# The last 32 tokens of the fetching block, held as four quarters of the channels over 128 partitions

## The chip, the cores and the metric

One core of a Trainium2 chip runs the whole kernel. The metric is the device time of one execution in microseconds (us). TensorE is called PE below (its weight loads PEld), VectorE DVE, ScalarE ACT, GpSimd POOL and SyncE SP, as in the profile.

## What is computed

One decoder block on 256 tokens of 1024 channels, in float32. A state-space mixer and attention are merged and added to x. Then comes the part that matters here, an expert layer (PEER): each token chooses 128 of 16384 experts (8 heads, 16 each), and each expert is one row of a table u and one row of a table v. After it a gated embedding and a final norm close the block:

```python
act = jax.nn.gelu(jnp.einsum('td,thkd->thk', hc, u_tab[ec]))
return jnp.einsum('thk,thkd->td', gc * act, v_tab[ec])
...
    e = p[i] @ ple_w_proj[i]
    x = x + jax.nn.sigmoid(rmsnorm(x, g_ple[i]) @ ple_w_gate[i]) * e
return rmsnorm(x, g_final)
```

## The kernel before

The 256 tokens are two blocks of 128. Block 0 is computed densely: all 16384 rows of u and then of v pass through PE, as 128 tiles of 128 rows each, and unchosen experts have weight zero. Block 1 fetches: for each of its tokens an indirect DMA from POOL's queue (`fetch_rows`, line 687) brings that token's 128 chosen rows, one to a partition.

The change lies in the second half, the sum over rows of v. `v_tile(e2)` fetches a dense tile on SP's queue and multiplies it with two matmuls into the PSUM banks `acc[0]`. `v_chosen(s)` fetches the rows of four tokens, 32q + s for q = 0 to 3, and gives each two matmuls of 512 columns: the weights are 32 columns wide with one column that is not zero, so token 32q + s is added to row s of column strip q of PE, and the four strips run side by side (`tile_position=(0, 32 * q)`). 32 calls cover block 1. A float32 matmul shows as two instructions in the profile. Tiles and rows share one ring of 18 buffers (`RING`), given out in program order.

The loop over the 128 tiles calls `v_chosen` after every third tile from tile 46 on (`ROWS_FROM`, `ROWS_EVERY`), 28 times. Beside tiles up to 61 it also has the selection jobs `g_step` of block 0 (16 small matmuls each, lines 956 and 957), at two tiles the projection `e_part` of the embedding, and from tile 64 on the loads of the gate weights. Four `v_chosen` calls are left behind the loop. They alternate with the five finishing steps of block 0: `turn_x` twice (transposes of x), `norm_x`, `gated` twice (a gate of 512 columns each: 8 matmuls, tanh, multiply-adds, the squares for the final norm) and `finish` (scaling and output DMA). Then `settle(1)` adds the sums of block 1 to x, and the same five steps run for block 1 with nothing beside them.

`rms` makes each reciprocal root: small DVE operations around one `pow` on POOL (line 1099), whose queue also issues the row fetches. PE's order is the program's (`in_turn`); the order on the other engines is set by the scheduler from its own simulated times, and `rms` runs under `tc.high_priority()`.

## Time and profile before

| what | us |
|---|---|
| median of 3 runs (lowest, highest) | 992.03 (991.92, 995.79) |
| the profiled execution, its own time | 990.05 |
| span of that execution, first to last instruction | 988.3 |
| busy in the span: PE, DVE, ACT, POOL | 922.6, 461.2, 160.6, 315.2 |
| loads on SP's queue q1 and on POOL's queue q0, MB | 178.02, 134.26 |

The span is what the trace shows; the execution's own time has 1.75 us around it. A busy PE includes waits inside a run of matmuls, so its share says little by itself; what ends a wait says more. Instructions are read with the line of the kernel, the operation, and what is written <- what is read.

### The profile page before, as it was taken

What the parts mean: (1) busy time and instruction counts of PE and PEld (TensorE: products, weight loads), DVE (VectorE), ACT (ScalarE), POOL (GpSimd) and SP (SyncE); (2) the same over time, 40 slices, a digit from 0 to 9 for tenths busy, and PEclk for the clock granted to TensorE, in tenths of its full rate; (3) what the DMA queues carried; (4) which work ended last, traced back from release to release, by engine and by line L of the source; (5) the groups of instructions that cost most, each with busy time, mean ns of one, the idle gap of its engine ahead of it and who ended that gap; (6) DMA issues with size and microseconds to landing.
All of it is one profiled execution on the core that took longest, in us unless ns stands there. A gap on an engine that the chain in (4) does not pass through costs nothing.

```text
span 988.3 us, 10506 instructions
## 1 busy us (share of the span) xinstructions
PE 922.6 (93%) x3594; PEld 495.0 (50%) x3594; DVE 461.2 (47%) x1338; ACT 160.6 (16%) x336; POOL 315.2 (32%) x353
## 2 busy tenths in 40 slices
PE   6889999999999999679999999889995999999996
PEld 5436777888756754234555545434431333233332
DVE  5787692322654789983466778752100000000023
ACT  6524442011321223201111000000000000000003
POOL 2022121011054532253323466533432443344611
PEclk9999999999999999879999999999998999999999
DMA  9333225922389999999999999999999999999931
GB/s 342 135 104 108 101 79 201 410 78 86 102 294 407 409 408 409 390 338 411 409 409 407 377 398 409 410 409 409 409 409 409 410 409 409 409 409 409 409 152 42
DMA packets 86948, 314.52 MB, mean 318 GB/s; under 512 B 9824, under 2 KB 9840, under 8 KB 86640
## 3 DMA queue, kind: packets, MB, share of 16 engines
q1 hardware_dynamic: 49392, 178.02, 46.8%
q0 software_dynamic: 36928, 134.26, 34.4%
q10 hardware_dynamic: 576, 1.59, 0.5%
q8 instruction: 28, 0.46, 0.2%
q14 instruction: 24, 0.20, 0.1%
HBM read 312.78 MB, written 1.05 MB: 318 GB/s over the span
## 4 chain that ended last, share of the span: by engine, by line
PE 65%; DMA 23%; DVE 8%; ACT 2%; issue 2%; POOL 0%; POOLq 0%; SPq 0%; DVEq 0%; ACTq 0%
PE sp L724 18%; PE va L1011 12%; DMA dn<-in_v 10%; DMA sel<-in_v,rowV 9%; PE va L1021 6%; PE q2p L773 5%; PE zp L126 5%; DMA dn<-in_u 3%; PE nat L452 3%; PE wop L126 3%; PE gp L1136 2%; PE psp L126 1%; PE pap L126 1%; PE gps L957 1%; PE gps L956 1%
## 5 line engine op out<-in xcount | busy, mean ns | idle before, releaser
L687 POOL DMA_INDIRECT sel<-in_urow,rowU x128 | 154.0, 1203 | 250.4 <-PE sp L724 81.5
L724 PE MATMUL sp<-dn,hn 128*128 128x512 f32 x512 | 228.7, 598 | 0.4 <-DMA dn<-in_u 0.2
L687 POOL DMA_INDIRECT sel<-in_v,rowV x128 | 120.3, 940 | 179.9 <-DMA sel<-in_v,rowV 70.4
L734 DVE SCALAR_TENSOR_TENSOR sel<-sel,h1n 128x1024 f32<-128x1024 f32 x128 | 154.6, 1250 | 43.6 <-DMA sel<-in_urow,rowU 29.6
L724 PEld LDWEIGHTS sp<-dn,hn 128*128 128x128 f32 x512 | 95.8, 192 | 109.2 <-issue 102.9
L1011 PE MATMUL va<-dn,SA 128*128 128x512 f32 x256 | 119.6, 605 | 7.8 <-DMA dn<-in_v 7.7
L1021 PE MATMUL va<-sel,C 128*32 128x512 f32 x512 | 99.2, 598 | 5.5 <-DMA sel<-in_v,rowV 5.4
L998 DVE TENSOR_TENSOR x_n<-x_n,va 128x512 f32<-128x512 f32 x4 | 2.7, 685 | 211.7 <-PE va L1011 211.7
L1011 PEld LDWEIGHTS va<-dn,SA 128*128 128x128 f32 x256 | 45.7, 191 | 68.6 <-issue 46.9
L1011 PE MATMUL va<-dn,SB 128*128 128x512 f32 x128 | 61.3, 624 | 10.1 <-DMA dn<-in_v 10.1
L1021 PEld LDWEIGHTS va<-sel,C 128*32 128x32 f32 x512 | 24.5, 109 | 72.5 <-issue 53.0
L126 PE MATMUL zp<-hT,nat 128*128 128x256 f32 x256 | 58.0, 382 | 0.5 <-DVE gat L549 0.5
L773 PE MATMUL q2p<-hn,dn 128*128 128x256 f32 x256 | 57.8, 379 | 0.0
L1011 PE MATMUL va<-dn,SC 128*128 128x512 f32 x128 | 57.8, 600 | 0.0
L726 ACT ACTIVATE sn<-sp,rst 128x512 f32<-128x512 f32 x32 | 22.0, 689 | 185.4 <-PE sp L724 185.3
L126 PEld LDWEIGHTS zp<-hT,nat 128*128 128x128 f32 x256 | 47.7, 190 | 8.3 <-DVE gat L549 0.9
L773 PEld LDWEIGHTS q2p<-hn,dn 128*128 128x128 f32 x256 | 47.5, 190 | 5.8
L452 PE MATMUL nat<-nat,hT 128*128 128x512 f32 x96 | 46.0, 633 | 2.8 <-ACT qk L457 2.8
L1011 PEld LDWEIGHTS va<-dn,SB 128*128 128x128 f32 x128 | 24.1, 197 | 47.0 <-issue 32.5
L943 DVE TENSOR_TENSOR ohl<-oq,gTl 128x512 f16<-128x512 f16 x32 | 13.5, 423 | 73.0 <-PE gps L956 72.8
L416 POOL TENSOR_TENSOR wc<-wc,ws 128x512 f32<-128x512 f32 x8 | 10.3, 1291 | 110.4 <-DVE ws L415 102.3
L1011 PEld LDWEIGHTS va<-dn,SC 128*128 128x128 f32 x128 | 23.5, 190 | 34.2 <-issue 34.2
(285 smaller groups left out, 1024.1 us busy)
## 6 DMA issues: line engine op xcount, KB each, us to landing
dn<-in_u SPq DMA_DIRECT2D x128, 512.0 KB, 11.0
dn<-in_v SPq DMA_DIRECT2D x128, 512.0 KB, 15.6
nat<-in_w_in SPq DMA_DIRECT2D x31, 512.0 KB, 3.3
dn<-in_wq SPq DMA_DIRECT2D x16, 512.0 KB, 10.1
nat<-in_wout SPq DMA_DIRECT2D x8, 512.0 KB, 10.2
g<-in_gate SPq DMA_DIRECT2D x8, 512.0 KB, 20.1
nat<-in_patt SPq DMA_DIRECT2D x4, 512.0 KB, 3.2
nat<-in_pssm SPq DMA_DIRECT2D x4, 512.0 KB, 7.2
```

What stands on the lines that cost most here:

```text
L126: nc.tensor.matmul(ps[:, :T], w[:, k, j * P:(j + 1) * P], a[:, k, :], start=(k == 0), stop=(k == kc - 1))
L416: nc.gpsimd.tensor_tensor(hc[:, :, 0, :], hc[:, :, 0, :], hs_[:, :, 1, :], ALU.subtract)
L452: nc.tensor.matmul(acc[t], hT[:, c, ts], pc[:, k, :], start=(c == 0), stop=(c == DC - 1))
L687: nc.gpsimd.indirect_dma_start(out=sel, out_offset=None, in_=src_d, in_offset=bass.IndirectOffsetOnAxis(ap=rows, axis=0))
L724: pe[0] = nc.tensor.matmul(ps, hn[:, c, :P], w[:, k, :], start=(c == 0), stop=(c == DC - 1))
L726: nc.scalar.activation(sn, ps, AF.Gelu_apprx_tanh, scale=rst2[:, 0:1])
L734: nc.vector.scalar_tensor_tensor(sel, sel, 1.0, h1n, ALU.mult, ALU.mult, accum_out=dots[:, j:j + 1])
L773: pe[0] = nc.tensor.matmul(ps[:, :T], w[:, k], hn[:, k], start=(k == 0), stop=(k == DC - 1))
L943: nc.vector.tensor_tensor(ol, oq, over(gTl, w), ALU.mult)
L1011: pe[0] = nc.tensor.matmul(acc[0][d], s_slot(e2), nat[:, d * 512:(d + 1) * 512], start=(e2 == 0), stop=(e2 == NE - 1))
L1021: pe[0] = nc.tensor.matmul(acc[1][d][32 * q:32 * q + 32, :], C3[:, 32 * t:32 * t + 32], rows[q][:, d * 512:(d + 1) * 512], start=(s == 0), ...
L1136: pe[0] = nc.tensor.matmul(ps, hf[:, c, ts], w[:, c % 2, :], start=(c == 0), stop=(c == DC - 1))
```

## The change

The last 32 tokens of block 1 (`LATE`) leave the groups. `v_chosen` now fetches for three strips, 96 tokens, and is called 23 times over the tiles from 46 on (`CHOSEN_BY`) and nine times behind the loop, beside the finishing steps of block 0. Then `settle(1)` and the five finishing steps of block 1 deal with 96 tokens; they stand among 32 calls of the new `v_late`, one step to every fourth call (`LATE_EVERY`). `v_late` fetches one token's rows and adds them with four matmuls of 256 columns, one to each column strip: quarter q of the channels of late token s lands in row 32q + s of a 256-wide sum. `late()` then finishes these 32 tokens in that shape: add, two transposes, gate (32 matmuls of 256 columns on four strips), final norm, scaling, four output DMAs. A norm now needs a sum over the four quarters, which is a matmul with the constant matrix `same`. What this shape needs of x, of the embedding and of the final gain (`x_q`, `e_q`, `g_q`) is made or loaded beside the dense tiles. One multiplication by the gain that ran on POOL for block 1 (line 1142) goes to DVE.

```diff
-ROWS_EVERY = 3
+LATE = 32
+NP = [P, P - LATE]
+CHOSEN_BY = 23
+Q_BY = 70
+LATE_EVERY = 4
...
         def v_chosen(s):
-            rows = [fetch_rows(v_rows, rowV[:, 32 * q + s:32 * q + s + 1]) for q in range(4)]
+            rows = [fetch_rows(v_rows, rowV[:, 32 * q + s:32 * q + s + 1]) for q in range(3)]
             with in_turn():
                 for d in range(2):
-                    for q in range(4):
+                    for q in range(3):
...
+        acc_l = psV1.tile([P, 512], F32, name="val")[:, :256]
+
+        def v_late(s):
+            t = P - LATE + s
+            rows = fetch_rows(v_rows, rowV[:, t:t + 1])
+            with in_turn():
+                for q in range(4):
+                    pe[0] = nc.tensor.matmul(acc_l[32 * q:32 * q + 32, :], C3[:, 32 * t:32 * t + 32],
+                                             rows[:, q * 256:(q + 1) * 256], start=(s == 0), stop=(s == LATE - 1),
+                                             tile_position=(0, 32 * q))
...
+            ps = psG.tile([P, 512], F32, name="ep", tag="gps")
+            with in_turn():
+                for k in range(2):
+                    for q in (2 * i, 2 * i + 1):
+                        pe[0] = nc.tensor.matmul(ps[32 * q:32 * q + 32, :256], pT[:, k, T - LATE:],
+                                                 w[:, k, q % 2 * 256:q % 2 * 256 + 256], start=(k == 0), stop=(k == 1),
+                                                 tile_position=(0, 32 * q))
+            qs = slice(64 * i, 64 * i + 64)
+            nc.scalar.activation(e_q[qs], ps[qs, :256], AF.Copy)
+
+        def x_quarters():
+            ps = psG.tile([P, 512], F32, name="xqp", tag="gps")
+            with in_turn():
+                for c in range(DC):
+                    q = c // 2
+                    pe[0] = nc.tensor.matmul(ps[32 * q:32 * q + 32, c % 2 * P:c % 2 * P + P], xT[:, c, T - LATE:], ident,
+                                             start=True, stop=True, tile_position=(0, 32 * q))
+            nc.scalar.activation(x_q, ps[:, :256], AF.Copy)
...
-            if e2 >= ROWS_FROM and (e2 - ROWS_FROM) % ROWS_EVERY == 0:
+            while chosen < (e2 + 1 - ROWS_FROM) * CHOSEN_BY // (NE - ROWS_FROM):
                 v_chosen(chosen)
                 chosen += 1
+            if e2 == Q_BY:
+                x_quarters()
...
+                for q in range(4):
+                    nc.sync.dma_start(g_q[32 * q:32 * q + 32], gfin_d[:, q * 256:(q + 1) * 256].to_broadcast([32, 256]))
+                same = eE.tile([P, 4, 32], F32, name="same")
+                nc.vector.tensor_reduce(same[:, 0, :], ident.rearrange("p (q i) -> p i q", i=32), AX.X, ALU.add)
+                nc.vector.tensor_copy(same[:, 1:, :], same[:, 0:1, :].to_broadcast([P, 3, 32]))
...
+                    ps = psE.tile([P, 512], F32, name="sqp", tag="X")
+                    with in_turn():
+                        pe[0] = nc.tensor.matmul(ps[:, 0:1], same.rearrange("p q i -> p (q i)"), sq_q[:, k:k + 1],
+                                                 start=True, stop=True)
+                    nc.vector.tensor_scalar(v, ps[:, 0:1], 1.0 / D, EPS, ALU.mult, ALU.add)
...
-            (nc.gpsimd if h == 0 and t else nc.vector).tensor_tensor(x_n[:, t, hs], x_n[:, t, hs], g_row[:, hs], ALU.mult)
+            nc.vector.tensor_tensor(x, x, g_row[:np_, hs], ALU.mult)
...
+        def late():
+            nc.vector.tensor_tensor(x_q, x_q, acc_l, ALU.add)
+            jq = eE.tile([P, 256], F32, name="jq")
+            ps = psE.tile([P, 512], F32, name="xqT", tag="X")
+            with in_turn():
+                for j in range(2):
+                    pe[0] = nc.tensor.transpose(ps[:, j * P:(j + 1) * P], x_q[:, j * P:(j + 1) * P], ident)
+            nc.scalar.activation(jq, x_q, AF.Square, accum_out=sq_q[:, 0:1])
+            hq = eE.tile([P, DC, LATE], F32, name="hq")
+            nc.vector.tensor_tensor(hq.rearrange("p (q j) i -> p q j i", j=2),
...
+            rms(2 * NT, r1, True)
+            pg = psE.tile([P, 512], F32, name="gpq", tag="A", bufs=2)[:, :256]
+            with in_turn():
+                for c in range(DC):
+                    for q in range(4):
+                        pe[0] = nc.tensor.matmul(pg[32 * q:32 * q + 32, :], hq[:, c, :],
+                                                 gate_w(c, q // 2)[:, q % 2 * 256:q % 2 * 256 + 256],
+                                                 start=(c == 0), stop=(c == DC - 1), tile_position=(0, 32 * q))
+            sg = eE.tile([P, 256], F32, name="sgq")
+            nc.scalar.activation(sg, pg, AF.Tanh, scale=r1)
+            nc.vector.scalar_tensor_tensor(sg, sg, 1.0, e_q, ALU.add, ALU.mult)
+            nc.vector.scalar_tensor_tensor(x_q, sg, 0.5, x_q, ALU.mult, ALU.add)
+            nc.scalar.activation(jq, x_q, AF.Square, accum_out=sq_q[:, 1:2])
+            nc.vector.tensor_tensor(x_q, x_q, g_q, ALU.mult)
+            rms(2 * NT + 1, r2, False)
+            nc.vector.tensor_scalar(x_q, x_q, r2, None, ALU.mult)
+            for q in range(4):
+                (nc.scalar if q % 2 else nc.sync).dma_start(out_d[P - LATE:, 1, q * 256:(q + 1) * 256],
+                                                            x_q[32 * q:32 * q + 32, :])
...
-        steps = [lambda: turn_x(0, 0), lambda: (turn_x(0, 1), norm_x(0)), lambda: gated(0, 0),
-                 lambda: gated(0, 1), lambda: finish(0)]
-        left = 32 - chosen
-        for i in range(max(left, len(steps))):
-            if i < left:
-                v_chosen(chosen)
-                chosen += 1
-            if i < len(steps):
-                steps[i]()
+        todo = steps(0)
+        while chosen < 32:
+            v_chosen(chosen)
+            chosen += 1
+            if todo:
+                todo.pop(0)()
         settle(1)
-        for h in range(2):
-            turn_x(1, h)
-        norm_x(1)
-        for h in range(2):
-            gated(1, h)
-        finish(1)
+        todo += steps(1)
+        for i in range(LATE):
+            v_late(i)
+            if todo and i % LATE_EVERY == LATE_EVERY - 1:
+                todo.pop(0)()
+        late()
```

`settle`, `squares`, `rms`, `turn_x`, `gated` and `finish` take only the first 96 partitions where they deal with block 1.

## Rows read from the trace of the kernel before

**Rows 1.** The page's part 2: the span in 40 equal slices of 24.7 us; the granted clock in tenths of full speed, and the GB/s that the DMA engines moved.

```profile
...
PEclk9999999999999999879999999999998999999999
...
GB/s 342 135 104 108 101 79 201 410 78 86 102 294 407 409 408 409 390 338 411 409 409 407 377 398 409 410 409 409 409 409 409 410 409 409 409 409 409 409 152 42
...
```

**Rows 2.** Busy time by windows around the end. Columns: the window in us, its length, busy us and instruction counts of PE, PEld, DVE, ACT and POOL, granted clock, DMA share, GB/s.

```profile
...
940.00:945.00 5.00, 5.00 (x23) 1.75 (x20) 1.46 (x7) 0.62 (x2) 2.46 (x3) 1.00 1.03 410
...
947.00:948.00 1.00, 1.00 (x3) 0.30 (x2) 0.00 (x0) 0.00 (x0) 0.00 (x0) 1.00 0.71 287
...
950.00:951.00 1.00, 1.00 (x4) 0.47 (x3) 0.00 (x0) 0.00 (x0) 0.00 (x0) 1.00 0.02 8
...
```

**Rows 3.** The row fetches of line 687 between 926 and 942 us: their durations in ns, the first and last start, and the time from issue to landing.

```profile
...
L687 POOL DMA_INDIRECT sel<-in_v,rowV x13: 936/936/938, 926.1 to 941.4; - x13
...
DMA to landing us min/median/max: 9.4/9.5/9.5
```

**Rows 4.** Timeline of POOL in the dense stage and at its end: start, length, line, operation, count, and in brackets the idle time before it and what ended that.

```profile
...
650.00 0.94 POOL L687 DMA_INDIRECT sel<-in_v,rowV  x1 [0.30 <-issue]
...
941.41 0.94 POOL L687 DMA_INDIRECT sel<-in_v,rowV  x1 [0.34 <-issue]
942.38 0.59 POOL L1099 TENSOR_TENSOR r_all<-v,mhalf 128x1 f32<-128x1 f32 x1
...
```

**Rows 5.** Timeline of PE from the last groups of rows to the transposes of block 1, columns as in rows 4.

```profile
...
938.00 4.60 PE L1021 MATMUL va<-sel,C 128*32 128x512 f32 x16
...
947.65 7.13 PE L1136 MATMUL gp<-g,hf 128*128 128x512 f32 x16
954.71 1.94 PE L1021 MATMUL va<-sel,C 128*32 128x512 f32 x16
956.59 7.13 PE L1136 MATMUL gp<-g,hf 128*128 128x512 f32 x16
963.56 1.04 PE L1115 MATMUL x2T<-ident,x_n 128*128 128x128 f32 x8
...
```

**Rows 6.** The chain of work that ended last, pieces in order of time around the first groups of rows: start, length, line, instructions.

```profile
...
677.43 1.87 PE va L1021 x16
679.30 5.35 PE va L1011 x12
...
```

**Rows 7.** Timeline of PE in the state-space stage: the outputs on two column strips (line 430), and what starts behind them.

```profile
...
67.10 1.06 PE L430 MATMUL yp<-wc,cblk 128*32 128x256 f32 x8
68.10 1.09 PE L477 MATMUL qkTp<-ident,qk 128*128 128x128 f32 x8
...
```

**Rows 8.** Groups of instructions by line, form and engine in the first 300 us: operands, count, busy us and mean ns of one, idle time before.

```profile
...
L549 DVE TENSOR_TENSOR gat<-zp,rbc 128x256 f32<-128x256 f32 x16 | 6.6, 416 | 22.8 <-PE zp L126 22.8
...
L259 ACT ACTIVATE xs<-xn 128x256 f32<-128x256 f32 x8 | 3.3, 414 | 0.2
...
L430 PEld LDWEIGHTS yp<-wc,cblk 128*32 128x32 f32 x64 | 3.2, 109 | 5.0 <-issue 3.5
...
L563 ACT ACTIVATE sgl<-glp 128x256 f32<-128x256 f32 x4 | 1.5, 383 | 15.2 <-PE glp L126 15.2
...
L259 ACT ACTIVATION_READ_ACCUMULATOR xs<-xn 128x1 f32 x8 | 1.5, 186 | 0.0
...
L637 DVE TENSOR_SCALAR hn<-xT,gains 128x256 f32<-128x256 f32 x4 | 1.4, 353 | 0.1
...
L139 PE MATMUL ss_ffn<-ones,sq 128*128 128x1 f32 x4 | 0.6, 255 | 1.0 <-ACT sq L144 1.0
...
L139 PEld LDWEIGHTS ss_ffn<-ones,sq 128*128 128x128 f32 x4 | 0.5, 190 | 1.1 <-ACT sq L144 1.1
...
```

**Rows 9.** Timeline of all engines behind the last gate of block 1, columns as in rows 4.

```profile
...
978.79 0.69 ACT L1138 ACTIVATE sg<-gp,r_all 128x512 f32<-128x512 f32 x1 [3.97 <-PE gp L1136]
979.51 0.69 DVE L1139 SCALAR_TENSOR_TENSOR sg<-sg,e_n 128x512 f32<-128x512 f32 x1 [5.45 <-ACT sg L1138]
...
981.03 0.63 ACT L1090 ACTIVATE junk<-x_n 128x512 f32<-128x512 f32 x1 [1.54 <-DVE x_n L1140]
...
983.85 0.72 ACT L1151 ACTIVATE x_n<-x_n,r_all 128x512 f32<-128x512 f32 x1 [2.10 <-DVE r_all L1102]
...
984.60 0.35 ACTq L1154 DMA_DIRECT2D out<-x_n  x1
```

**Rows 10.** Timeline of PE: a selection job (its first instruction, and the tile behind its sixteenth), and the tiles behind the longest wait of the dense stage.

```profile
...
688.28 0.22 PE L956 MATMUL gps<-ohl,o 128*128 128x64 f16 x1
...
689.25 3.67 PE L1011 MATMUL va<-dn,SA 128*128 128x512 f32 x8
...
763.39 7.84 PE L1011 MATMUL va<-dn,SB 128*128 128x512 f32 x12 [9.94 <-DMA dn<-in_v]
...
```

**Rows 11.** Busy time by windows, columns as in rows 2, around that wait and in the stage in which PE waits for single rows.

```profile
...
755.00:760.00 5.00, 0.00 (x0) 0.00 (x0) 0.00 (x0) 0.00 (x0) 0.77 (x1) 0.81 1.02 409
760.00:763.00 3.00, 0.00 (x0) 0.00 (x0) 0.00 (x0) 0.00 (x0) 0.00 (x0) 0.50 1.03 411
...
938.00:943.00 5.00, 5.00 (x21) 1.84 (x20) 0.00 (x1) 0.37 (x1) 3.90 (x5) 1.00 1.03 410
...
```

**Rows 12.** Timeline of DVE: the input of the `pow` of block 0's norm, and what waited for its result.

```profile
...
934.36 0.15 DVE L1098 TENSOR_SCALAR v<-v 128x1 f32<-128x1 f32 x1
943.00 0.16 DVE L1100 TENSOR_TENSOR rs<-r_all 128x1 f32<-128x1 f32 x1 [8.49 <-POOL r_all L1099]
...
```

More of the change, by code (lines that the diff above doesn't have):

```diff
@@ L1070, in block_kernel @@
                 nc.sync.dma_start(pT, pT_d)
+                e_q = eE.tile([P, 256], F32, name="e_q")
+                x_q = eE.tile([P, 256], F32, name="x_q")
+                g_q = eE.tile([P, 256], F32, name="g_q")
+                for q in range(4):
[3 more added lines that the diff above has]
+                nc.vector.tensor_copy(same[:, 1:, :], same[:, 0:1, :].to_broadcast([P, 3, 32]))
                 g_row = eE.tile([P, D], F32, name="g_row")
@@ L1086, in block_kernel @@
         sq_s = eE.tile([P, 2 * NT, 2], F32, name="sq_s")
+        sq_q = eE.tile([P, 2], F32, name="sq_q")
         def squares(t, h, i):
             junk = eE.tile([P, 512], F32, name="junk")
-            nc.scalar.activation(junk, x_n[:, t, h * 512:(h + 1) * 512], AF.Square, accum_out=sq_s[:, i, h:h + 1])
+            np_ = NP[t]
+            nc.scalar.activation(junk[:np_], x_n[:np_, t, h * 512:(h + 1) * 512], AF.Square,
+                                 accum_out=sq_s[:np_, i, h:h + 1])
         def rms(i, r, half):
+            np_ = NP[i % NT] if i < 2 * NT else P
             with tc.high_priority():
-                v = eE.tile([P, 1], F32, name=f"v{i}")
-                rs = eE.tile([P, 1], F32, name=f"rs{i}")
-                nc.vector.tensor_tensor(v, sq_s[:, i, 0:1], sq_s[:, i, 1:2], ALU.add)
-                nc.vector.tensor_scalar(v, v, 1.0 / D, EPS, ALU.mult, ALU.add)
-                nc.gpsimd.tensor_tensor(r, v, mhalf[:, 0:1], ALU.pow)
+                v = eE.tile([P, 1], F32, name=f"v{i}")[:np_]
+                rs = eE.tile([P, 1], F32, name=f"rs{i}")[:np_]
+                r = r[:np_]
+                if i < 2 * NT:
+                    nc.vector.tensor_tensor(v, sq_s[:np_, i, 0:1], sq_s[:np_, i, 1:2], ALU.add)
+                    nc.vector.tensor_scalar(v, v, 1.0 / D, EPS, ALU.mult, ALU.add)
+                else:
+                    ps = psE.tile([P, 512], F32, name="sqp", tag="X")
+                    k = i - 2 * NT
+                    with in_turn():
+                        pe[0] = nc.tensor.matmul(ps[:, 0:1], same.rearrange("p q i -> p (q i)"), sq_q[:, k:k + 1],
+                                                 start=True, stop=True)
+                    nc.vector.tensor_scalar(v, ps[:, 0:1], 1.0 / D, EPS, ALU.mult, ALU.add)
+                nc.gpsimd.tensor_tensor(r, v, mhalf[:np_, 0:1], ALU.pow)
                 nc.vector.tensor_tensor(rs, r, r, ALU.mult)
@@ L1127, in norm_x, with gate_w @@
             rms(t, r_all[:, t:t + 1], True)
+        def gate_w(c, h):
+            return gate[4 * h + c // 2].rearrange("p (k n) -> p k n", k=2)[:, c % 2, :]
         def gated(t, h):
-            ts = slice(t * P, (t + 1) * P)
+            np_ = NP[t]
+            ts = slice(t * P, t * P + np_)
             hs = slice(h * 512, (h + 1) * 512)
-            ps = psE.tile([P, 512], F32, name="gp", tag="A", bufs=2)
+            ps = psE.tile([P, 512], F32, name="gp", tag="A", bufs=2)[:np_]
             with in_turn():
                 for c in range(DC):
-                    w = gate[4 * h + c // 2].rearrange("p (k n) -> p k n", k=2)
-                    pe[0] = nc.tensor.matmul(ps, hf[:, c, ts], w[:, c % 2, :], start=(c == 0), stop=(c == DC - 1))
-            sg = eE.tile([P, 512], F32, name="sg", bufs=2)
-            nc.scalar.activation(sg, ps, AF.Tanh, scale=r_all[:, t:t + 1])
-            nc.vector.scalar_tensor_tensor(sg, sg, 1.0, e_n[:, t, hs], ALU.add, ALU.mult)
-            nc.vector.scalar_tensor_tensor(x_n[:, t, hs], sg, 0.5, x_n[:, t, hs], ALU.mult, ALU.add)
+                    pe[0] = nc.tensor.matmul(ps, hf[:, c, ts], gate_w(c, h), start=(c == 0), stop=(c == DC - 1))
+            sg = eE.tile([P, 512], F32, name="sg", bufs=2)[:np_]
+            x = x_n[:np_, t, hs]
+            nc.scalar.activation(sg, ps, AF.Tanh, scale=r_all[:np_, t:t + 1])
+            nc.vector.scalar_tensor_tensor(sg, sg, 1.0, e_n[:np_, t, hs], ALU.add, ALU.mult)
+            nc.vector.scalar_tensor_tensor(x, sg, 0.5, x, ALU.mult, ALU.add)
             squares(t, h, NT + t)
-            (nc.gpsimd if h == 0 and t else nc.vector).tensor_tensor(x_n[:, t, hs], x_n[:, t, hs], g_row[:, hs], ALU.mult)
+            nc.vector.tensor_tensor(x, x, g_row[:np_, hs], ALU.mult)
         def finish(t):
+            np_ = NP[t]
             r2 = r_all[:, NT + t:NT + t + 1]
@@ new lines, in late @@
+        def late():
[8 more added lines that the diff above has]
+            nc.vector.tensor_tensor(hq.rearrange("p (q j) i -> p q j i", j=2),
+                                    ps[:, :256].rearrange("p (j q i) -> p q j i", j=2, q=4),
+                                    gp.rearrange("p (q j) -> p q j", j=2).unsqueeze(3).to_broadcast([P, 4, 2, LATE]),
+                                    ALU.mult)
+            r1, r2 = (r_all[:, 2 * NT + i:2 * NT + i + 1] for i in range(2))
+            rms(2 * NT, r1, True)
[17 more added lines that the diff above has]
+                                                            x_q[32 * q:32 * q + 32, :])
@@ L1175, in layout @@
+        assert not todo
+        late()
 def layout(inputs):
```

24 lines of the change are left out of this document (15 added, 9 removed).

## The prediction

> **What bounds the kernel now.** I read the slices of the page first, then the windows around the end, then the timelines of each engine there. From the middle of the span on, the traffic stands at 407 to 411 GB/s in most slices, dips in four and falls for good only in the last two, while TensorE's clock stays at its upper level but for short dips [rows 1]. So the second half is paced by DMA: each tile or row fetch moves 128 x 1024 x 4 B = 0.524 MB, 1.28 us at 409 GB/s. The end is different. The traffic is still 410 GB/s at 940 to 945 us, is down to 287 at 947, and the last bytes come at 950 to 951 [rows 2]; the last row fetch is issued at 941.41 and lands 9.4 to 9.5 us later, at 950.9 [rows 3, 4]. From there to the end of the span are 988.3 - 950.9 = 37.4 us with no load left to hide them. The reader is to see in the PE timeline what fills them: gates of block 0, the last group of rows at 954.71, gates of block 0 again, then the whole finish of block 1: transposes at 963.56, 14 us of gate matmuls, then an elementwise chain [rows 5, 9].
>
> **What is removed from behind the last row.** Both gate halves of block 0 and both of block 1 (7.06 us of PE each, as from 947.65 to 954.71 [rows 5]) now stand among the fetches; only 32 tokens, spread as four quarters of the channels over 128 partitions, are finished behind the last row. The sum needs two things: when the last row has gone through PE, and how long the new tail is.
>
> **When the last row is through: the DMA side.** Bytes of rows and tiles are the same, 128 row fetches each time, moved from the dense stage (112 before, 69 after) to behind it (16 before, 59 after). New ahead of the last row are the outputs of block 0 (0.524 MB, 1.28 us) and of 96 tokens of block 1 (0.96 us), which were written behind it before, and four loads of the quartered gain (0.13 MB, 0.3 us): 2.6 us. So the last row lands at 950.9 + 2.6 = 953.5 if the queues stay full, and its own matmuls (0.5, below) with a wait of 0.3 end at 954.3. Will a stage of rows alone stay full? In the stretch 926 to 942 every fetch was a row, 1.28 us apart (0.94 of work and 0.34 idle), landing steadily 9.4 to 9.5 us after issue at 410 GB/s [rows 2, 3, 4]. POOL's shortest step is 0.94 + 0.30 = 1.24 us [rows 4], so it has only 0.04 us a fetch to spare. Four new-placed `pow` operations (norm and finish of either block) of 0.59 us plus 0.3 each take 3.6 us from it; the 9.4 us in flight absorb that, and I cost it at nothing. Without that cover it is 3.6 us. What a waiting `pow` would cost is a rival below. All tiles stand ahead of them on SP's queue, and ACT's issues take 0.35 us each [rows 9], so the moved output DMAs block no load.
>
> **The PE side.** The group of four rows, 16 instructions on four column strips, takes 1.87 us; with three strips each strip still has its four instructions, so a group of three rows costs 1.87 as well, 32 times: 0.62 a row instead of 0.47. A tile takes 5.35 / 3 = 1.783 [rows 6]. A late row is 8 instructions of 256 columns over four strips, two a strip. No row shows this; the nearest is the state-space output, 8 instructions of the same shape on two strips, four a strip, in 68.10 - 67.10 = 1.0 us, 0.25 an instruction [rows 7]. So a late row is 2 x 0.25 = 0.5 us; halving the 512-column group gives 0.47 as the low bound; weight loads strictly one after another, 8 x 0.109 [rows 8], give 0.87 as the high one. I take 0.5, since the same strips overlap in both rows. From the first group at 677.43 PE then has: 81 tiles 144.4; 32 groups 59.8; four selection jobs of 0.97 [rows 10], 3.9; the embedding projection, 16 instructions at 5.35 / 12, 7.1; its quartered copy and the quartered x, three sets like rows 7, 3.0; 16 transposes at 0.13 [rows 5], 2.1; four gates 28.2; 32 late rows 16.0. That is 264.5 us. To it comes one idle stretch of 9.9 with a slow restart of 7.84 - 5.35 = 2.5, which the burst of eight gate-weight loads caused and will cause again [rows 10]: 276.9, so 954.3. The late rows and the quartered copies, 19 us, are new in it; with them the two sides meet. Each will hold up the other now and then (14 us of gates at once leave about 15 of the 18 ring slots landed and unused), so I set the last row's end at 955.5.
>
> **The new tail.** The add from PSUM 0.42, as the 128x256 of VectorE; Square and its read 0.41 + 0.19; the sum over quarters as a 1-column matmul, 0.45 (0.26 and a weight load of 0.19); with 0.2 of handoffs 1.65 until gates may start, the two transposes and their 0.42 copy running beside it [rows 8, 9]. The gate is 64 instructions on four strips, 16 a strip: 16 x 0.25 = 4.0 (bounds 3.7 by rows 6, 7.0 by loads one after another) and 0.1 to start. So 5.75 to its end. From the end of the last gate before, at 978.79, to the end of the span it was 9.5 us [rows 9]. With 256 columns in place of 512, tanh loses 0.31, the two multiply-adds 0.54, Square 0.22, the scaling 0.37 [rows 8, 9]; the gain no longer stands between the sum and its `pow` (0.5 less); the 1-column matmul in place of an add costs 0.4, a second output issue per queue 0.35. That is 8.3. The tail is 14.1 us, the span 955.5 + 14.1 = 969.6, 18.7 less than before.
>
> Added work hidden elsewhere: the `same` matrix, e_q, x_q and their copies, some 2 us of ACT and DVE in stretches where both are near idle, 2 us on the path if that cover went; four SP issues of 0.35, 1.4 us, under up to 18 tiles in flight. The multiplication moved from POOL to VectorE, some 0.69 as its like in rows 9, lies among the rows.
>
> **The clock, and a rule against the change.** The granted clock fell to 0.50, 1.2 of 2.4 GHz, after PE had nothing at all from 753 to 763, and 12 matmuls then took 7.84 us; while PE waited for each row at 938 to 943 it stayed at 1.00 [rows 10, 11]. The Trainium skill, TensorE: Matmul & The Clock Gate, section HAM oscillation, warns that bursts that wait for their DMA each time let the clock fall back; late rows are such bursts. By the trace at 938 to 943 nothing changes and the span is 969.6; by the rule the tail runs at half clock and it is 974.9.
>
> **Rivals.**
> 1. *The clock falls among the late rows*, since 0.5 us of work stands in each 1.28 us, for longer than before. The rows in reach speak against it: 1.87 us of work in 4.6 at 938 to 943 left it at 1.00 [rows 5, 11]. Price: gate + 4.0, last row, transposes and 1-column matmuls + 1.3: 5.3, time 978.6.
> 2. *PE becomes the bound* with late rows at 0.87: 32 x 0.37 = 11.8 on PE, and the gate 7.0: + 3.0. As PE was level with DMA, all of it is seen: 13.6 with the 1.2 us of slack that I gave, time 987. For it: no margin; against: the strips overlap in two shapes.
> 3. *POOL waits inside its queue (the other side).* POOL is in order; if the `pow` of block 0's finish stands ahead of the fetches that follow it in the program, these wait for gates on PE. The first four groups behind the last tile, with the turns and gates between them, take PE some 23 us, the chain to `pow` 3.7, while only about 5 unlanded rows are under way: some 21 us without DMA; block 1's finish adds 7. 28 us against 18.7 gained: 9.3 slower, time 1001. It decides from 18.7 us of idle DMA on. Against it: the `pow` of block 0's norm, ahead of eight fetches in the program, ran at 942.38 behind all of them, though its input was there from 934.5 [rows 4, 12]. A part of it, one `pow` some fetches too early, 5 to 12 us, is likelier: about 981.
>
> **How the numbers follow.** The profiled execution took 990.05, 1.75 above its span; the median of the runs shown, 992.03, is 1.98 above that. So 969.6 gives 971.35 and, as median, 973.3. Chances: forecast 0.62, clock 0.08, PE bound 0.09 (half of it in between, about 980), POOL in part 0.14, POOL in full 0.07. The forecast's own range is 966 (outputs absorbed, a tail 3 us shorter) to 978; the range 966 to 985 holds all but the full cases of rivals 2 and 3. Faster by over 0.5% (5 us, about what a measurement of this kernel can tell) 0.88, within 0.05, slower 0.07.
>
> **What would show it.** Right: traffic near 409 GB/s until about 951 us; 59 row fetches in a row at 1.28 us; late rows of 0.5 us on PE; under 15 us from the last row to the end; clock 1.00 throughout. Wrong: gaps in POOL's fetches ended by VectorE's `v`; traffic that dips among the gates; late rows over 0.8 us; 0.50 in the last 20 us.

## The result, and the profile after

The changed kernel took 987.19 us (median of 10 runs, 982.17 to 989.52), the kernel before 992.74 (10 runs, 989.26 to 995.91): a ratio of 0.995 (0.9928 to 0.9971). Forecast were 973.3 and a range of 966 to 985. The profiled execution took 989.52, the longest of the ten; its span is 987.8, and the forecast span was 969.6.

The page's part 2 of the changed kernel, columns as in [rows 1]:

```profile
...
PEclk9989999999999999879999999999997999999889
...
GB/s 344 147 99 110 90 86 213 409 61 86 109 294 408 409 407 409 392 316 409 409 408 409 382 396 409 409 408 409 409 398 409 403 374 394 410 409 375 310 360 55
...
```

The traffic dips where it was to stand at 409, and the clock is under its upper level near the end. Busy time by windows there, columns as in [rows 2]:

```profile
...
913.00:920.00 7.00, 7.00 (x31) 2.45 (x32) 1.39 (x2) 1.35 (x3) 1.76 (x2) 1.00 0.67 268
920.00:926.00 6.00, 6.00 (x52) 2.38 (x49) 0.83 (x3) 0.06 (x1) 4.47 (x6) 1.00 0.77 236
930.00:946.00 16.00, 10.08 (x32) 2.11 (x32) 0.62 (x3) 1.03 (x4) 10.85 (x12) 0.58 1.02 399
...
```

Among the gates of block 0 the traffic is 268 and 236 GB/s. From 930 to 946 it is full again, yet PE runs 32 instructions in 16 us, and its clock stands at 0.58. The timeline of PE shows these instructions; the columns are those of [rows 4]:

```profile
...
929.00 0.62 PE L1178 MATMUL x2T<-ident,x_n 96*128 96x96 f32 x4 [1.46 <-issue]
930.73 0.59 PE L1039 MATMUL val<-sel,C 128*32 128x256 f32 x2 [1.10 <-issue]
932.19 2.73 PE L1039 MATMUL val<-sel,C 128*32 128x256 f32 x7 [0.87 <-issue]
935.75 1.30 PE L1039 MATMUL val<-sel,C 128*32 128x256 f32 x3 [0.83 <-issue]
937.88 1.05 PE L1039 MATMUL val<-sel,C 128*32 128x256 f32 x2 [0.83 <-issue]
...
946.05 0.55 PE L1178 MATMUL x2T<-ident,x_n 96*128 96x96 f32 x4
...
967.52 7.11 PE L1039 MATMUL val<-sel,C 128*32 128x256 f32 x128
...
976.13 3.66 PE L1245 MATMUL gpq<-g,hq 128*32 128x256 f32 x64
...
```

Four late rows, 32 instructions, lie between the transposes at 929.00 and those at 946.05. Where nothing disturbs them, 128 instructions take 7.11 us (967.52), so 32 should take 1.8. Here they come in pieces of one to nine. The starts are 1.46, 2.13 or 3.56 us apart, all near multiples of 0.71 us, and the idle time before each piece ended by nothing that the profile shows ("issue"). In the runs below I call this *pieces*. ScalarE, too, follows PE late. Its copies of the transposes of 892.31 and of 929.00 (recorded ends 892.97 and 929.62):

```profile
...
900.58 0.37 ACT L1186 ACTIVATE hf<-x2T,gains 128x128 f32<-128x128 f32 x1 [8.57 <-PE va L1027]
...
945.08 0.34 ACT L1186 ACTIVATE hf<-x2T,gains 128x96 f32<-128x96 f32 x1 [14.58 <-PE val L1039]
...
```

They start 7.6 and 15.5 us after them. The Trainium skill, Perfetto Trace Analysis, section Summary: the profiler window per engine type, says that TensorE's record has an estimated end and leaves out the propagation of its semaphore. This trace shows the 7.6 and 15.5 us; whether PE's signal came late or ScalarE's own instruction it does not show.

PE loses time before any late row, too. A group of three rows is 12 instructions and takes 1.8 us where nothing holds it (half of 3.66 at 888.72); the one at 896.40 takes 4.62. Its weight loads wait three times (0.76, 0.29 and 0.44 us), by the profile for rows, yet POOL had issued its three fetches by 881.9, and a fetch landed 9.5 us after its issue in the kernel before [rows 3]. PE's timeline up to the first gate of block 0:

```profile
...
888.72 3.66 PE L1027 MATMUL va<-sel,C 128*32 128x512 f32 x24
892.31 0.66 PE L1178 MATMUL x2T<-ident,x_n 128*128 128x128 f32 x4
...
896.40 4.62 PE L1027 MATMUL va<-sel,C 128*32 128x512 f32 x12
901.00 7.13 PE L1203 MATMUL gp<-g,hf 128*128 128x512 f32 x16
...
```

POOL's timeline in the same stretch:

```profile
...
919.17 0.94 POOL L692 DMA_INDIRECT sel<-in_v,rowV  x1 [5.24 <-PE va L1027]
...
926.67 0.59 POOL L1161 TENSOR_TENSOR r_all<-v,mhalf 128x1 f32<-128x1 f32 x1
...
939.78 0.58 POOL L1161 TENSOR_TENSOR r_all<-v,mhalf 96x1 f32<-96x1 f32 x1
940.53 0.99 POOL L692 DMA_INDIRECT sel<-in_v,rowV  x1 [0.18 <-issue]
...
```

It stops for 5.24 us before 919.17, until PE gives a slot of the full ring free, then fetches every 1.25 us until 940.53. The two `pow` (926.67, 939.78) fit in between without a wait.

Rows end at 967.52 + 7.11 = 974.6 in place of 955.5. The tail behind them is 987.8 - 974.6 = 13.2 in place of 14.1. So the whole miss, 19.1 us, lies ahead of the last row's end.

### The profile page after: what moved, and what is told of

Its sections match the earlier page's. It is cut to its first block, busy times and chain, and to the rows that moved or that the text cites. A ratio compares the mean times of both kernels' runs of the same rounds, so it can differ in the third digit from the quotient of the medians.

```text
span 987.8 us, 11007 instructions
## 1 busy us (share of the span) xinstructions
PE 918.2 (93%) x3824; PEld 498.7 (50%) x3824; DVE 467.3 (47%) x1356; ACT 163.8 (17%) x344; POOL 319.7 (32%) x354
## 4 chain that ended last, share of the span: by engine, by line
PE 75%; DMA 12%; DVE 8%; issue 3%; ACT 2%; POOL 0%; SPq 0%; POOLq 0%; DVEq 0%; ACTq 0%
PE sp L729 19%; PE va L1017 17%; DMA dn<-in_v 9%; PE q2p L778 5%; PE zp L131 5%; PE va L1027 5%; PE gp L1203 3%; PE wop L131 3%; PE nat L457 3%; PE val L1039 2%; PE psp L131 1%; PE pap L131 1%; PE gps L962 1%; PE gps L961 1%; DMA dn<-in_u 1%
## 5 line engine op out<-in xcount | busy, mean ns | idle before, releaser
L692 POOL DMA_INDIRECT sel<-in_urow,rowU x128 | 156.6, 1224 | 248.6 <-PE sp L729 78.4
L692 POOL DMA_INDIRECT sel<-in_v,rowV x128 | 122.6, 958 | 195.6 <-PE va L1017 82.0
L1004 DVE TENSOR_TENSOR x_n<-x_n,va 128x512 f32<-128x512 f32 (+1 forms) x4 | 2.6, 682 | 171.2 <-PE va L1017 170.5
L1027 PE MATMUL va<-sel,C 128*32 128x512 f32 x384 | 63.9, 598 | 0.0
L1027 PEld LDWEIGHTS va<-sel,C 128*32 128x32 f32 x384 | 15.4, 109 | 43.8 <-issue 40.8
```

The costliest lines, as they stand in the source:

```text
L692: nc.gpsimd.indirect_dma_start(out=sel, out_offset=None, in_=src_d, in_offset=bass.IndirectOffsetOnAxis(ap=rows, axis=0))
L1027: pe[0] = nc.tensor.matmul(acc[1][d][32 * q:32 * q + 32, :], C3[:, 32 * t:32 * t + 32], rows[q][:, d * 512:(d + 1) * 512], start=(s == 0), ...
```

## The experiments

The 18 runs came in five groups, each on a chip of its own; I number the chips in that order. The chip of the runs of the result isn't recorded. All ratios are to the kernel before on the same chip. The first theory (pieces come where transposes and gates stand among single rows) had as rivals traffic, the number of instructions, and the full ring.

**First chip: is it the steps among the rows, the instructions, the bytes or the ring?**

*Block 1's steps behind the last late row.*

```diff
-        todo += steps(1)
         for i in range(LATE):
             v_late(i)
-            if todo and i % LATE_EVERY == LATE_EVERY - 1:
-                todo.pop(0)()
...
+        for step in todo + steps(1):
+            step()
```

> The five steps of block 1 (transposes, norm, two gate halves, finish) stand behind the last of the 32 late rows instead of behind every fourth of them. Theory A (TensorE falls behind when it is fed the sixteen narrow instructions of a late row while the traffic is full): the rows that came in pieces in the changed kernel, four in 15 us, come in pieces still, over 1.5 us a row wherever the traffic is above 390 GB/s, and the span is over 1000 us. Theory B (it is the transposes and gates between the rows that make TensorE wait): with none of them between, every late row goes through at the pace at which rows land, 1.25 to 1.3 us, the last one ends near 964, and the span is 964 + 1.5 + 14.3 + 13.5 = about 993. Theory C (only the gates of block 0, 16 us in one go, matter, because the ring fills and the fetches stop): the fetches still stop for 5 us near 913, and rows run as in theory B.

Measured: 992.63 (10 runs), ratio 1.0017 (1.0003 to 1.003). PE, among rows alone:

```profile
...
929.16 0.59 PE L1039 MATMUL val<-sel,C 128*32 128x256 f32 x2 [0.83 <-issue]
...
942.65 6.35 PE L1039 MATMUL val<-sel,C 128*32 128x256 f32 x49 [0.82 <-issue]
...
```

Pieces stand from 926 to 943, and again from 949 to 958, with no transpose or gate among the rows. That theory falls. The rows end at 964.9; the steps behind them cost the rest.

*Half the instructions of late rows 1 to 30 (two strips of four).*

```diff
-                for q in range(4):
+                for q in range(2 if 0 < s < LATE - 1 else 4):
```

> Of each late row but the first and the last, only the strips of two of the four quarters are multiplied (half of the channels of these 30 rows are left out): half of the instructions, the same fetches, transposes and gates. Theory A: the four rows that took 15 us take 4 us or less, the fetches do not wait for TensorE near 943, and the time is 972 to 980 us. Theories B and C: the pieces and their gaps stay, 12 us or more for these four rows, and the time is within 3 us of the changed kernel's 987.

Measured: 980.58 (4 runs), ratio 0.9898 (0.9878 to 0.9918). The time lies between the two that were expected. Pieces stay, from 925.7 to 941. They last as long as before. With half the instructions a row, about five rows pass in them (21 instructions) in place of four, which may be part of why less time is lost.

*Half of the bytes of each late row* (the first half of its channels, by an index doubled beforehand; the two upper strips multiply it once more).

```diff
-            rows = fetch_rows(v_rows, rowV[:, t:t + 1])
...
+            nc.gpsimd.indirect_dma_start(out=rows[:, :512], out_offset=None, in_=v_half,
+                    in_offset=bass.IndirectOffsetOnAxis(ap=rowV2[:, s:s + 1], axis=0))
...
```

> Each late row is fetched with half of its channels (2 KB a partition instead of 4; the second half of the channels is then multiplied with the first half's values). As many fetches and TensorE instructions, but the traffic of this stage falls to about 210 GB/s, since the issue of a fetch takes 1.24 us whatever it moves. Theory A: no pieces, each late row 0.47 us, and the time is 968 to 978 us. Theory B: the pieces stay, since transposes and gates stand where they stood: 980 us or more. Theory C: the fetches still stop near 913 for 5 us, rows run as in theory A.

Measured: 982.91 (4 runs), ratio 0.9925 (0.9901 to 0.995). Busy time by a window in the pieces, columns as in [rows 2]:

```profile
...
930.00:941.00 11.00, 5.50 (x13) 1.86 (x14) 0.14 (x1) 0.00 (x0) 7.30 (x8) 0.50 0.70 203
...
```

13 PE instructions in 11 us at 203 GB/s: full traffic is not the cause.

*Each gate in halves of eight instructions, a group or four rows between them.*

```diff
-            return [..., lambda: gated(t, 0), lambda: gated(t, 1), ...]
+            return [..., lambda: gate_part(t, 0, 0), lambda: gated(t, 0),
+                    lambda: gate_part(t, 1, 0), lambda: gated(t, 1), ...]
```

> Each gate half of 7.1 us is given out in two parts of four accumulation steps, 3.5 us, with a group of rows (or four late rows) between them; nothing else differs. Theory C: the ring never fills, the 5 us without a fetch near 913 are gone, the last row is through 6 to 12 us sooner, and the time is 975 to 981 us. Theory A: TensorE falls behind as before at the late rows, the time is 983 to 989 us. Theory B: two more places where other work stands between rows, 987 us or more.

Measured: 987.73 (10 runs), ratio 0.9986 (0.9966 to 1.0007). POOL's longest stop is 2.86 us in place of 5.24; the pieces stand from 924.7 to 939. The ring is not their cause either, and with it all three theories of this group have fallen.

**Second chip: place in the instruction stream, block 0's finish, who fetches.** One run each.

*64 small matmuls more, long before, so that PE's later instructions move on in its stream.*

```diff
+            if e2 == W0 + 1:
...
+                    for _ in range(64):
+                        pe[0] = nc.tensor.matmul(ps[:, :64], iot4[:, :, 0], iot4[:, :64, 0], start=True, stop=True)
```

> Sixty-four small matmuls (128 instructions with their weight loads) are added near 720 us, where TensorE later waits about 10 us for the gate weights; nothing else changes. In the four experiments before, the stretch in which TensorE's instructions come 0.7 us and more apart began at the same place of its instruction stream, whatever stood there. Theory D (TensorE's instructions themselves come too late, at a place of the stream): the stretch begins 128 instructions earlier in the work, among the groups of three rows near 922 us or it is gone, and late rows 4 to 7 take about 2 us. Theory F (row fetches through POOL's queue, or another thing that hangs on the work itself): it stays at late rows 4 to 7, 12 to 15 us, time as the changed kernel's, 987.

*`finish(0)` behind the last late row.*

```diff
-        todo = steps(0)
+        todo = steps(0)[:4]
...
+        finish(0)
         late()
```

> The finish of block 0 (norm, scaling and its two output DMAs of 256 KB) stands behind the last late row. Theory E (the outputs of block 0, which start at 928 us, where the stretch begins, hold TensorE up): the gaps at late rows 4 to 7 are gone, the rows end near 962, and the time is about 977 with the finish added to the tail's side work. Theories D and F: the gaps stay, 12 to 15 us for these rows, time 986 to 990.

*Late rows as plain tiles on SyncE's queue* (32 consecutive tiles, not the chosen rows).

```diff
-            rows = fetch_rows(v_rows, rowV[:, t:t + 1])
+            rows = fetch_dense(v_d[s])
```

> The 32 late rows are fetched by SyncE as plain tiles of the same size, and from fixed places, not the chosen ones (their values are therefore other ones); POOL then issues nothing among them. Theory F (fetches through POOL's queue hold TensorE up): no gaps, 0.5 us a late row, the time falls to about 972. Theory D: the gaps stay where they are in the stream, 12 to 15 us for rows 4 to 7.

*One strip of four in late rows 1 to 30.*

```diff
-                for q in range(4):
+                for q in range(1 if 0 < s < LATE - 1 else 4):
```

> Of late rows 1 to 30 one quarter of the channels alone is multiplied: 4 instructions a row with the weight loads, in place of 16; same fetches. Theory A, which the run with two strips spoke against: no gaps at all. Theory D: the gaps last as long in instructions as before, some 50 of them 0.3 us each, and so reach over more rows; with 4 instructions a row TensorE still follows the fetches at 1.25 us a row, and the rows end near 964, the time is about 977. Theory F: gaps in the same fetches, near 926 to 942 us, whatever the number of instructions.

Measured: 973.42, 976.47, 972.67 and 977.42, the kernel before 986.89. None of the four has pieces, so nothing here tells what removes them; the chip itself became the suspect. Two things can be read, each from single runs. A quarter of the PE work in late rows 1 to 30 gave no shorter time (977.42 against 973.42 with all of it, the stream shifted), so nothing shows PE as the bound of an undisturbed run. And moving `finish` behind the rows did not help (976.47).

**Third chip: the unaltered kernel again.**

> The changed kernel itself, unaltered, once more. The last four experiments ran on another chip than the four before them, and none of them shows TensorE's instructions coming in pieces, not even the one whose edit stands far from that place. Theory G (the pieces belong to the chip on which the kernel runs, not to the kernel alone): on a chip without them the unaltered kernel takes 973 to 977 us, its late rows 4 to 7 about 2 us; on a chip with them 985 to 989. Theory D alone (the place in the instruction stream, which the added matmuls moved): 985 to 989 with the pieces at late rows 4 to 7, whatever the chip.

> The kernel with 64 small matmuls added near 720 us, once more, beside the unaltered one on the same chip. Theory G: within 2 us of the unaltered kernel beside it, on either kind of chip; where there are pieces they start near the same instruction number or the same row. Theory D: 10 us or more faster than the unaltered one.

> The gate halves given out in two parts, on the same chip as the unaltered kernel. If no pieces disturb TensorE, this edit is tested alone: the fetches then wait less for the ring while the gates of block 0 run (they waited 5.3 us in all in the kernel with the added matmuls), the last row is through 3 to 5 us sooner, near 955, and the time is 2 to 5 us under the unaltered kernel's. With pieces: within 2 us of it.

Measured: the unaltered kernel 975.16 (4 runs, 971.35 to 978.74), ratio 0.9853 (0.9814 to 0.9891); with the stream shifted 976.31 (4), 0.9856; with gates in halves 975.9 (4), 0.986. No pieces in any of them. This is the cleanest result of the study: the same kernel has a span of 972.6 here and 987.8 in the profile of the result. PE of the unaltered kernel on the third chip:

```profile
...
886.76 3.66 PE L1027 MATMUL va<-sel,C 128*32 128x512 f32 x24
890.35 0.66 PE L1178 MATMUL x2T<-ident,x_n 128*128 128x128 f32 x4
...
893.38 1.93 PE L1027 MATMUL va<-sel,C 128*32 128x512 f32 x12
895.24 7.13 PE L1203 MATMUL gp<-g,hf 128*128 128x512 f32 x16
...
928.63 0.64 PE L1039 MATMUL val<-sel,C 128*32 128x256 f32 x8 [1.67 <-DMA sel<-in_v,rowV]
931.32 1.08 PE L1039 MATMUL val<-sel,C 128*32 128x256 f32 x8 [2.05 <-DMA sel<-in_v,rowV]
...
933.61 9.19 PE L1203 MATMUL gp<-g,hf 128*96 128x512 f32 x16
...
958.88 0.64 PE L1039 MATMUL val<-sel,C 128*32 128x256 f32 x8 [0.57 <-DMA sel<-in_v,rowV]
...
961.01 3.66 PE L1245 MATMUL gpq<-g,hq 128*32 128x256 f32 x64
...
```

Each late row is whole, and what ends its wait is its own data. The pieces are gone, and ScalarE no longer follows late; its copies behind the transposes that end at 891.01 and 926.11:

```profile
...
891.04 0.37 ACT L1186 ACTIVATE hf<-x2T,gains 128x128 f32<-128x128 f32 x1 [2.68 <-PE x2T L1178]
...
926.15 0.34 ACT L1186 ACTIVATE hf<-x2T,gains 128x96 f32<-128x96 f32 x1 [0.47 <-PE x2T L1178]
...
```

What is left of the miss shows in the windows and at POOL:

```profile
...
913.00:920.00 7.00, 7.00 (x57) 2.56 (x56) 1.31 (x4) 0.72 (x2) 5.07 (x6) 1.00 0.69 216
920.00:926.00 6.00, 4.57 (x73) 2.73 (x65) 2.96 (x10) 2.73 (x7) 4.89 (x6) 1.00 1.01 333
...
930.00:934.00 4.00, 2.49 (x17) 0.80 (x18) 0.00 (x0) 0.00 (x0) 3.06 (x5) 0.63 1.03 419
934.00:938.00 4.00, 4.00 (x6) 1.23 (x6) 1.16 (x6) 0.34 (x1) 3.21 (x4) 0.52 1.03 410
...
```

```profile
...
913.41 0.93 POOL L692 DMA_INDIRECT sel<-in_v,rowV  x1 [3.80 <-PE va L1027]
...
```

The ring is full behind block 0's gates, POOL stops 3.80 us, and the traffic is 216 and 333 GB/s. Against 409 that is (193 x 7 + 76 x 6) / 409 = 4.4 us of DMA. Behind this gap PE waits 1.67 and 2.05 us for single rows, the clock falls to 0.63 and 0.52, and the gate at 933.61 takes 9.19 in place of 7.11.

With gates in halves (the third kernel of this group) POOL stops for no more than 0.87 us there, and traffic ends at 952, as the forecast had it. It gained nothing:

```profile
...
931.83 5.43 PE L1206 MATMUL gp<-g,hf 128*96 128x512 f32 x6 [3.35 <-DVE hf L1184]
...
953.67 3.66 PE L1039 MATMUL val<-sel,C 128*32 128x256 f32 x64
959.69 0.44 PE L1241 MATMUL xqT<-ident,x_q 128*128 128x128 f32 x2 [2.36 <-DVE x_q L1236]
...
```

The rows end at 957.3, but a gate half waited 3.35 us for its input and ran at half clock, and the tail's first add stood 2.36 us behind the elementwise work of block 1's finish on VectorE.

**Fourth chip: is it the work or its place, and who fetches?**

*Gates in halves, block 1's norm behind the first half, a step to every third late row* (shown against the kernel with gates in halves).

```diff
-LATE_EVERY = 4
+LATE_EVERY = 3
-            return [lambda: turn_x(t, 0), lambda: (turn_x(t, 1), norm_x(t)), lambda: gate_part(t, 0, 0),
+            return [lambda: turn_x(t, 0), lambda: turn_x(t, 1), lambda: (gate_part(t, 0, 0), norm_x(t)),
```

> Gate halves in two parts as before, the norm of a block behind its first gate part (so that VectorE's copies for the gate no longer queue behind the power that POOL works off late), and the steps of block 1 behind every third late row, so that its finish is done before the last row. On a chip without pieces: the 2.4 us that the tail waited for the finish of block 1, the 3.4 us for the copies and the half clock of the tail's gate (1.7 us) go; the last row is through near 953, and the time is 966 to 970 us, 5 to 9 under the unaltered kernel. If the order of these steps does not matter: 974 to 976. On a chip with pieces: 980 to 987.

> The changed kernel unaltered, on the same chip as the three others of this call. Theory G: either 971 to 979 us without pieces, or 982 to 990 with pieces at late rows 4 to 7; nothing between.

> The kernel with 64 small matmuls (128 instructions) near 720 us. If this chip shows pieces in the unaltered kernel: a cause in the place of the instruction stream moves them by 128 instructions towards the start of the work, to the groups before the late rows; a cause in the work itself leaves them at late rows 4 to 7. If not: within 3 us of the unaltered kernel.

> Late rows fetched by SyncE from fixed places (their values are other ones). If this chip shows pieces in the unaltered kernel: if row fetches through POOL's queue take part in the cause, there are none here, 972; if not, pieces as in the unaltered kernel, 985. On a chip without pieces: 972, as before.

Measured: reordered 981.5 (4 runs), ratio 0.9887 (0.9847 to 0.9927); unaltered 985.09 (7 runs), 0.9935 (0.9901 to 0.997); stream shifted 985.83 (one run); rows by SyncE 974.1 (one run); the kernel before 992.07. The pieces are back in the first three. PE with the stream shifted:

```profile
...
928.30 2.51 PE L1039 MATMUL val<-sel,C 128*32 128x256 f32 x6 [1.00 <-issue]
...
```

They stand at the same late rows as without the 128 instructions (64 matmuls and their weight loads) ahead of them. So they hang on the work and not on a place in the stream. With the late rows issued by SyncE, PE, ScalarE and the windows:

```profile
...
891.75 0.66 PE L1178 MATMUL x2T<-ident,x_n 128*128 128x128 f32 x4
...
924.34 0.55 PE L1178 MATMUL x2T<-ident,x_n 96*128 96x96 f32 x4
...
927.59 0.64 PE L1039 MATMUL val<-dn,C 128*32 128x256 f32 x8 [0.36 <-DMA dn<-in_v]
...
931.45 0.64 PE L1039 MATMUL val<-dn,C 128*32 128x256 f32 x8 [1.94 <-DMA dn<-in_v]
...
```

```profile
...
895.36 0.37 ACT L1186 ACTIVATE hf<-x2T,gains 128x128 f32<-128x128 f32 x1 [3.07 <-PE va L1027]
...
924.92 0.34 ACT L1186 ACTIVATE hf<-x2T,gains 128x96 f32<-128x96 f32 x1
...
```

```profile
...
924.00:934.00 10.00, 6.42 (x80) 2.60 (x74) 2.13 (x11) 2.21 (x8) 0.54 (x1) 0.91 1.03 411
...
```

Whole rows, at 411 GB/s, on a chip where the other three kernels have pieces; bytes, ring and PE's work are the same. And this execution is no lucky one: while POOL still fetched groups of rows, ScalarE's copy came 2.95 us behind its transposes (their end is 892.41). POOL's last fetch ended at 908.6, and the next such copy came 0.03 us behind (924.89). So what goes with POOL's row fetches takes part in the pieces and in the late copies. This run alone can't part POOL's issuing from the scattered reading that it brings, since SyncE's tiles are consecutive, nor from POOL's queue to the DMA engines; the last run bears on the reading.

**Fifth chip: must POOL issue without a break?**

*Two POOL multiplies of 128 x 512 behind every fourth late fetch.*

```diff
...
+            if s % 4 == 3:
+                for _ in range(2):
+                    with tc.issue_after(lastp[0].ins):
+                        lastp[0] = nc.gpsimd.tensor_tensor(pause, pause, pause, ALU.mult)
```

> The changed kernel unaltered, control of the two others. 971 to 979 us on a chip without pieces, 982 to 993 on one with them.

> Gate halves in two parts, norm behind the first part, a step of block 1 behind every third late row. On a chip without pieces 966 to 970 us, with the last row through near 953; on one with pieces 978 to 983, as the time before. If the order of the steps is worth nothing where no pieces are: 974 to 976.

> Behind every fourth late fetch POOL multiplies a spare 128x512 tile twice, about 2.6 us by the same operation elsewhere, so its fetches come in fours with a pause. Theory H (on some chips POOL's issuing of row fetches without a break holds up TensorE's instructions, and they flow again 1 to 2 us after it stops): with the pauses no stretch of pieces is longer than 5 us, late rows 4 to 7 take under 6 us in place of 15. The fetches themselves lose up to 8 x 2.6 = 21 us, so the time says nothing. If the pieces are not POOL's doing: 12 us and more for these four rows, across the pauses. On a chip without pieces this run says nothing of them.

Measured: unaltered 986.26 (10 runs), ratio 0.9943 (0.9918 to 0.9968); reordered 983.41 (6 runs), 0.9908 (0.9872 to 0.9943); with pauses 993.21 (one run); the kernel before 992.34. POOL and PE with the pauses:

```profile
...
926.88 2.16 POOL L1043 TENSOR_TENSOR pause<-pause 128x512 f32<-128x512 f32 x2
...
```

```profile
...
930.76 1.08 PE L1046 MATMUL val<-sel,C 128*32 128x256 f32 x8 [2.58 <-DMA sel<-in_v,rowV]
...
936.55 1.08 PE L1046 MATMUL val<-sel,C 128*32 128x256 f32 x8 [0.28 <-DMA sel<-in_v,rowV]
...
962.38 0.59 PE L1046 MATMUL val<-sel,C 128*32 128x256 f32 x3 [0.80 <-issue]
...
```

Late rows 4 to 11, of which the first four lay wholly or in part in pieces in every run before with POOL's fetches on such a chip, are whole, each in 0.64 us or, at half clock, 1.08, and most waits end by their data. Rows 4 to 7 took 6.9 us (under 6 were expected), 3.0 of them waits. The reading is as scattered as before. One stretch of pieces of some 3 us remains, at 962.4, between two pauses. So breaks in POOL's issuing take most of the pieces away, but cost more in fetches than they return (324 GB/s from 927 to 945). Beside this one run, the place where the pieces end supports it: on the first chip 1.4 us behind POOL's last fetch ahead of a stop with block 1's steps behind the rows (941.28, and 942.65 on PE), 2.1 us with half the bytes, 1.5 us with gates in halves. In the first of these runs the pieces that came back at 949 end the same way, 1.5 us behind the next stop (952.12, and 953.62 on PE).

## Why the prediction was wrong

**The step that failed** is the one that joined the two sides: "Each will hold up the other now and then ..., so I set the last row's end at 955.5". The 1.2 us given for it measured 955.5 + 19.1 - 954.3 = 20.3 in the profiled execution. The runs split the 19.1.

1. *Pieces and late starts, 13.1 us, and 2.0 unexplained.* The same kernel ends its rows at 959.5 without them (third chip) and at 974.6 with them, 15.1 us later. Of these, 2.0 stood already at the end of the dense stage (888.72 against 886.76), and no run says why. At the first gate of block 0 it was 5.8 (901.00 against 895.24): 2.7 of the 3.8 in between are the group of rows of 4.62 us, 1.93 on the third chip, though its fetches began no more than the same 2.0 apart (878.49 against 876.53). The other 9.3 came behind that gate, among the late rows. The medians differ by less, 12.0 (987.19 and 975.16), since the profiled execution was the longest of its ten. The forecast had taken for granted that PE runs an instruction when its data are there. The rows it leaned on for a stage of rows alone [rows 2, 3, 4] show POOL fetching unbroken as well, but there PE had 16 instructions for four rows and waited for each row's data [rows 5]; a late row asks for twice as many as each of these. No row of before shows a piece or a late copy; there ScalarE started 0.03 us behind the transposes that end at 938.07:

```profile
...
938.10 0.37 ACT L1122 ACTIVATE hf<-x2T,gains 128x128 f32<-128x128 f32 x1 [3.98 <-PE x2T L1115]
...
```

   That the kernel before never has them is not shown: one trace of it was read, and its chip isn't recorded.
2. *The ring and the clock, 4.0 us.* With no pieces the rows end at 959.5. The forecast reckoned with 15 of 18 slots landed and unused behind 14 us of gates and gave 1.2 us for all such hold-ups; the ring ran full, and 4.4 us of DMA were lost. Part of this lay in the margins; the clock added 2.1.

Without pieces the forecast held: 975.16 against 973.3, inside its range, and 14.1 us faster than before against 18.7, with the rows' end 4.0 later and the tail 1.0 shorter than forecast. With pieces 5.6 us were left. That they would come could not be read from the trace of before, and they were seen on some chips alone: whether the range held hung on the chip, of which the forecast knew nothing.

**The other steps.** A late row was put at 0.5 us; 7.11 / 16 = 0.44, and 1.87 / 4 = 0.47 between the starts at 942.72 and 944.59 of the third chip's run, at or under the low bound. The tail was put at 14.1; it is 13.2, of it 5.2 to the gate's end (5.75) and 8.0 behind it (8.3), the gate 3.66 (4.0). The `pow` operations on POOL did cost nothing. A stage of rows alone stayed near full, 399 GB/s in the pieces and 419 and 410 on the third chip.

**The rivals.** The first, the clock, came in part: 0.58 in the trace of the result, while PE's instructions came in pieces, and 0.52 among whole rows on the third chip. It was priced at 5.3 us; there it took 2.1 from one gate, and the tail's gate ran at the upper level (961.01, 3.66). In another execution on that chip, of the kernel with the stream shifted, it did not:

```profile
...
963.63 5.35 PE L1252 MATMUL gpq<-g,hq 128*32 128x256 f32 x64
...
```

That is 1.7 us more. The Trainium skill, TensorE: Matmul & The Clock Gate, section HAM oscillation, which spoke against the change, was right on the fall; the trace of before, on which I set the rule aside, had 1.87 us of work in each 4.6 at 938 to 943 [rows 5, 11], while here rows of 0.6 us came after waits of 1.67 and 2.05. The second rival, PE as the bound, needed late rows of 0.87; whole ones took 0.44 to 0.47, and the run with a quarter of the work was no faster. The third, POOL held in its queue by a `pow`, was not seen. POOL did wait for PE, 5.24 and 3.80 us, but for a ring slot.

## What to carry to other kernels

A stage can be bound by something that no wait in the profile names, though data and engine are free: "issue" before short pieces on PE, and copies that start microseconds after the matmuls they wait for. Look for both where GpSimd fetches rows without a break, also in the stretches that a forecast leans on, and time the kernel on more than one chip. When a block of matmuls moves among fetches, count ring slots against its length: 14 us of gates are 11 fetches of 1.28 us, beside 7 in flight (9.5 us to land), and the ring of 18 stood full and cost 4.4 us of transfer. The reordered version was 3.6 and 2.9 us under the unaltered one on the two chips where both ran; both had pieces, and it wasn't run on a chip without them. The ranges of its runs lie apart from the unaltered ones on the first of these chips and overlap on the second.

## What the runs showed of the hardware

PE's instructions came near multiples of 0.71 us apart, for 13 to 17 us, while POOL issued row fetches; in the same stretch of the profiled execution ScalarE followed PE by 15.5 us, elsewhere by 0.03 or 0.04. It happened on three of five chips and in the profile of the result, at 203 GB/s as at 399, and not with the rows issued by SyncE. One mark tells the two kinds of execution apart before any late row: the first copy of block 0's transposes starts 1.8 to 7.7 us after them in the profile of the result and in the traces of all eleven experiments on the three chips, the one with SyncE's late rows among them, and 0.03 or 0.04 us after them in those of all seven on the other two chips and in the trace of before. The kernel before, too, was slower on the three chips (990.33, 992.07 and 992.34) than on the other two (986.89 in one run, and 989.25); whether it loses something of this kind isn't shown. What POOL's issuing shares with PE's instructions or signals stays open, and so does why some chips show none; each chip ran one group, at one time, so a chip and a time can't be told apart.
